# Hybrid decoder block: mLSTM values copied into the load tiles, and priority for the copies that empty the projection banks

## The chip, the cores and the metric

The kernel runs on one core of a Trainium2 chip. Its time is the device time of one execution in microseconds (us), as the median of several runs; lower is better. A profiled execution, one of its own, gives the instructions of each engine with their times: TensorE (PE, with its weight loads as PEld), VectorE (DVE), ScalarE (ACT), GpSimdE (POOL), and SyncE (SP), which here only issues transfers (DMA).

## The reference, cut to what matters

One decoder layer over 2048 tokens of width 1024, all in float32. One combined projection of the normalised input gives what two mixers need:

```python
h = modulate(rms_norm(x, g_pre_mix), shift_m, scale_m)
q_a, k_a, v_a, q_m, k_m, v_m, o_m, i_m, f_m, g_a, g_m = split(h @ w_in)
q_a, k_a = rope(q_a), rope(k_a)
y_a = sliding_window_attention(q_a, k_a, v_a, sinks)        # window 128, 8 query and 2 key heads of 64
q_m, k_m = silu(causal_conv(q_m, k_m))
h_m = mlstm_chunkwise(q_m, k_m, v_m, i_m + b_i, f_m + b_f)  # 4 heads of 128, values v_m
y_m = sigmoid(o_m) * head_layer_norm(h_m)
merged = sigmoid(g_a) * (y_a @ W_A) + sigmoid(g_m) * (y_m @ W_B)
x = x + gate * rms_norm(merged @ w_out);  then the same sandwich around a SwiGLU feed-forward
```

## The kernel before

The tokens are worked on in four blocks of 512 (`TB`), numbered 0 to 3, two of them to a superblock; a block has four token tiles of 128 (`NT`). Every product in float32 is made of three products of split operands (a high and a low part each), which `mm3` issues. The high part of a weight is a ScalarE copy (`split`, L264 and L267, L1744 in `split_unit`), the low part a VectorE subtraction (L268, L1745). Sums stand in banks of PSUM: four named acc for the projections, four named mix for everything smaller (transposes, attention, mLSTM).

Queries (`evac_q`, 512 columns), keys with attention values and mLSTM gates (`evac_kv`, 264 columns) and mLSTM values (`vm`, 512 columns) are projected by `token_group`: it takes the four acc banks at once, one for each token tile, goes through the eight slices of the weights in four pieces, and after the last piece calls `evac` for each token tile, which copies the bank to SBUF. The order in a superblock is: queries, keys and values of its first block (in the first superblock queries and keys of block 0 come in a part of its own, `first_block`, whose instructions are kept in the order written), then keys, queries and values of its second block. After that come the other columns (`om`, `qk`, `ga`, `gm`), by fast products of both blocks at once (`pair_parts`), whose results are sums of seven products and which again use the acc banks.

What becomes of the copies:

- Queries: the copy (L813) goes to a tx tile, VectorE turns it (rotary, L790 to L793), TensorE transposes it later (`q_stream`), and GpSimdE's queue stores it to DRAM (L806).
- Keys: the copy (L840) goes to a tx tile, for block 0 to an ld tile; the keys are turned, transposed in `k_stream` and stored (L833), the attention values are stored directly (L853) and as a difference to the tile before (L851), all on GpSimdE's queue.
- mLSTM values: the copy (L870) goes to a tx tile, and SP's queue stores it to DRAM (L871). The mLSTM loads it from there when its chunk's turn comes (L1084).

Tiles that share a tag share a fixed number of places in SBUF. tx has nine of them, for the copies above, for VectorE's work on them, for weights of the conditioning (`ada_stream`, L476) and much else. ld has four, `kvp.tile([P, 512], ...)`; besides the keys of block 0 they hold the queries and keys that the mLSTM loads for a chunk (L1079, L1082; the first at 374.6 us). A tile's place is given on when all that read it are through, a transfer out of it included.

The order of the instructions on an engine is not the order written, but for `first_block`. The kernel's own planner weaves work into the projections: generators (attention, gates, rotary parts, `hsums`, whose L575 and L576 split sums after a copy by transfer, L569) are given due times in its own count of TensorE time (`now`, `spawn`, `tick`). The framework then schedules what was written: it goes through a model of the chip in time, and each engine takes, of the instructions whose inputs and places are ready in the model, the one with the highest priority, which by default is the one written first. On the chip each engine then goes through its list in that order and waits where the model was too quick.

Of the kernel before, what the change touches and what calls it, by code (L numbers as in the profile page):

```python
# [19 lines left out]
P = 128  # L20
# [24 lines left out]
L_LOAD, L_HP2, L_HC = 5000.0, 1000.0, 3000.0  # L45
L_TANH, L_CONV, L_HD = 1500.0, 4000.0, 5000.0
L_LATE = 2500.0
L_KV0 = 0.0
L_HS2 = 4000.0
L_REST = (2000.0, 1800.0, 2500.0, 2500.0)  # L50
# [23 lines left out]
def decoder_block(ctx: ExitStack, tc: tile.TileContext, a: dict, out: bass.AP, dbg=None):  # L74
# [19 lines left out]
    V, A, T, Q = (InOrder(e) for e in (nc.vector, nc.scalar, nc.tensor, nc.sync))  # L94
# [19 lines left out]
    def nm(s):  # L114
        uid[0] += 1
        return f"{s}{uid[0]}"
# [7 lines left out]
    def tx(shape, dtype=F32):  # L124
        return tpool.tile(shape, dtype, tag="tx", name=nm("tx"), bufs=9)
# [88 lines left out]
    def transpose(o, i):  # L214
        now[0] += 110.0
        k = i.shape[0]
        T.transpose(o, i, ident[:k, :k])  # L217

    def spawn(gen, delay=0.0):
        st = [now[0] + delay, gen, False]  # L220
        streams.append(st)
        return st
# [116 lines left out]
    def token_group(srcs, nk, n, lhs, evac, pair_heads=False, stagger=1, store=None, kept=False):  # L339

        acc = []
        srcs = list(srcs)
        held = []

        def make(si, k0, kc):
            def mms(wt):
                if not acc:
                    acc.extend(acc_tile() for _ in range(NT))
                held.append((wt, k0, kc))
                if len(srcs) - stagger <= si < len(srcs) - 1:  # L350
                    return
                for t in range(NT):
                    for w_, k0_, kc_ in held:
                        for j in range(kc_):
                            kk = k0_ + j
                            mm3(acc[t][:, :n], lhs(kk, t), (w_[0][:, j, :], w_[1][:, j, :]), kk == 0, kk == nk - 1)
                            yield
                    if si == len(srcs) - 1:
                        evac(t, acc[t])
                held.clear()  # L360
            return mms

        for si, (raw, view, k0, kc) in enumerate(srcs):
            if kept:
                def ready(raw=raw, q=view):
                    return tuple(v.rearrange("p (k c) -> p k c", k=2) for v in raw.tile[q])
                yield Part(raw, ready, make(si, k0, kc))
                continue
            part = piece(raw, view, [kc, n], make(si, k0, kc), pair_heads)
            if store:  # L370
                def prep(do=part.prep, si=si, kc=kc):
                    made = do()
                    for i, v in enumerate(made):
                        nc.sync.dma_start(W_D[store][:, si, i, :].rearrange("p (k c) -> p k c", k=kc), v.bitcast(F32))
                    return made
                part.prep = prep
            yield part

    def srcs_rows(w, nk, c0):
        for k0 in range(0, nk, 4):  # L380
            kn = min(4, nk - k0)
            raw = raw_rows(w, k0, kn, c0)
            for j in range(0, kn, 2):
                yield raw, (lambda t, j=j: t[:, j:j + 2, :]), k0 + j, 2
# [350 lines left out]
    def ld(shape, dtype=F32):  # L735
        t = kvp.tile([P, 512], dtype, tag="ld", name=nm("ld"), bufs=4)
        return t.rearrange("p (k c) -> p k c", k=shape[0])
# [31 lines left out]
    def superblock(sb):  # L769
# [3 lines left out]
        def lhs_h(b):  # L773
            def lhs(kk, t):
                return tuple(p_[:, kk % 4, t * P:(t + 1) * P] for p_ in HC[f"{kk // 4 + 1}{b % 2 + 1}"])
            return lhs


        def rope(raw, heads, b, t):
            sin, cos = tables[sb]  # L780
            t += (b % 2) * NT
            W = heads * HD
            raw = raw[:, :W]
            src = raw.rearrange("p (h u f) -> p h u f", u=2, f=32)
            cb = cos[:, t, :].unsqueeze(1).to_broadcast([P, heads * 2, 32])
            sb_ = sin[:, t, :].unsqueeze(1).unsqueeze(1).to_broadcast([P, heads, 2, 32])
            z = tx([P, 512])
            zz = z[:, :W].rearrange("p (h u f) -> p h u f", u=2, f=32)
            rr = raw.rearrange("p (h f) -> p h f", f=32)
            V.tensor_tensor(zz, src[:, :, ::-1, :], sb_, op=ALU.mult)  # L790
            V.tensor_tensor(rr, rr, cb, op=ALU.mult)
            V.tensor_tensor(src[:, :, 0, :], src[:, :, 0, :], zz[:, :, 0, :], op=ALU.subtract)
            V.tensor_tensor(src[:, :, 1, :], src[:, :, 1, :], zz[:, :, 1, :], op=ALU.add)  # L793
            return raw, z

        def q_stream(b, t, yz):
            yield L_ROPE
            y, z = yz
            pt = mix_tile()
            for j in range(GQ):  # L800
                transpose(pt[:, j * P:(j + 1) * P], y[:, j * P:(j + 1) * P])
            hi, lo = z.bitcast(F32R), y.bitcast(F32R)
            A.activation(hi, pt, AF.Copy, scale=HD ** -0.5)
            V.scalar_tensor_tensor(lo, pt, HD ** -0.5, hi.bitcast(F32), op0=ALU.mult, op1=ALU.subtract)
            for i, q in enumerate((hi, lo)):
                G.dma_start(at_d[b * NT + t][:, i * 512:(i + 1) * 512], q.bitcast(F32))  # L806
# [3 lines left out]
        def evac_q(b):  # L810
            def evac(t, ps):
                raw = tx([P, 512])
                A.copy(raw, ps)  # L813
                R["qk"].append(spawn(q_stream(b, t, rope(raw, HQ, b, t))))
            return evac

# [6 lines left out]
        def k_stream(n, yz):  # L823
            yield L_ROPEK
            y, z = yz
            pt = mix_tile()
            transpose(pt[:, :P], y)
            kk = z[:, P:3 * P].bitcast(F32R).rearrange("p (i k) -> p i k", i=2)
            A.copy(kk[:, 0, :], pt[:, :P])
            V.tensor_tensor(kk[:, 1, :], pt[:, :P], kk[:, 0, :].bitcast(F32), op=ALU.subtract)  # L830
            for n_, u in ((n, 1), (n + 1, 0)):
                if n_ < S // P:
                    G.dma_start(at_d[n_][:, AT_K:AT_V].rearrange("p (i u k) -> p i u k", i=2, u=2)[:, :, u, :], kk.bitcast(F32))  # L833

        def evac_kv(b):
            before = [v_last]

            def evac(t, ps):
                raw = ld([1, 512])[:, 0, :] if b == 0 else tx([P, 392])
                A.copy(raw[:, :264], ps[:, :264])  # L840
                v, dv = raw[:, 128:256], raw[:, 264:392]
                n = b * NT + t
                y = rope(raw, HKV, b, t)
                for i in range(2):
                    A.copy(gt[:, t, 32 * i:32 * i + 4], raw[:, 256 + 4 * i:260 + 4 * i])
                V.tensor_tensor(dv, v, before[0], op=ALU.subtract)
                before[0] = v
                if t == NT - 1:
                    A.copy(v_last, v)
                    before[0] = v_last  # L850
                G.dma_start(at_d[n][:, AT_V + P:], dv)  # L851
                if n + 1 < S // P:
                    G.dma_start(at_d[n + 1][:, AT_V:AT_V + P], v)  # L853
                R["qk"].append(spawn(k_stream(n, y)))
            return evac
# [10 lines left out]

        def vm(b):
            def evac(t, ps):
                v = tx([P, 512])
                A.copy(v, ps)  # L870
                nc.sync.dma_start(vm_d[b][:, t, :], v)  # L871
            if b > 1:
                yield from token_group(kept_weights("vm"), KD, 512, lhs_h(b), evac, kept=True)
            else:
                yield from token_group(srcs_rows(w_in, KD, C_VM), KD, 512, lhs_h(b), evac, store="vm" if b else None)
# [477 lines left out]
        if sb == 0:  # L1353
            raws, rotated = {}, {}

            def late_q(t):
                yield from q_stream(b0, t, rope(raws[t], HQ, b0, t))

            def q_raw(t, ps):
                raws[t] = tx([P, 512])  # L1360
                A.copy(raws[t], ps)
                if t > 1:
                    R["qk"].append(spawn(late_q(t), L_KV0 + L_LATE * (t - 1)))

# [871 lines left out]
def build(nc, aps, out):  # L2236
    with tile.TileContext(nc, schedule_with_timeline_sim=True) as tc, ExitStack() as ctx:
        decoder_block(ctx, tc, aps, out[0])
# [16 lines left out]
```

## Time and profile before

| | |
|---|---|
| median of 3 runs | 2659.16 us (2657.73 to 2660.38) |
| profiled execution | 2668.66 us, span 2667.0 us |
| granted TensorE clock, mean | 0.994 |
| busy: PE, DVE, ACT, POOL | 2615.5, 1937.2, 1281.9, 300.3 us |
| DMA | 532.97 MB, mean 200 GB/s |

The profile page gives the busy time of each engine, the span in 40 slices, the chain of work that ended last, and the costliest groups of instructions. Views of the trace add the order in time of each engine's instructions (timeline: start and duration in us, engine, line, operation, tiles written and read; in brackets the idle time of the engine just before and what ended it), who waited for whom, and the busy time, the granted clock of TensorE and the busy share of the 16 DMA engines in chosen windows. A line such as L870 is line 870 of the kernel before. L212 is the helper that issues the matmuls, L217 the one for transposes; L90 is a helper for what is kept in program order. An "issue" as what ended a wait means that the view shows nothing that the engine waited for.

### The profile page before, as it was taken

How to read it: one execution, taken by the hardware profiler on the slowest of the kernel's cores; microseconds unless marked ns; L12 is line 12 of the kernel's file. 1: busy time of each engine (PE TensorE's matmuls, PEld its weight loads, DVE VectorE, ACT ScalarE, POOL GpSimd, SP SyncE). 2: the span in 40 equal slices, each digit the busy share in tenths (PEclk: the TensorE clock that was granted, in tenths of full speed). 3: DMA queues.
4: the chain of work that ended last, by engine and by line, in shares of the span. 5: the costliest groups of instructions: out<-in, count | busy, mean ns of one | idle time of the engine just before them, and what ended most of it. 6: DMA issues, size and time to landing. Idle time of an engine off the chain costs nothing.

```text
span 2667.0 us, 36229 instructions
## 1 busy us (share of the span) xinstructions
PE 2615.5 (98%) x12546; PEld 2145.8 (80%) x12546; DVE 1937.2 (73%) x3758; ACT 1281.9 (48%) x2531; POOL 300.3 (11%) x473
## 2 busy tenths in 40 slices
PE   8999999999989999999999999999999999999998
PEld 6877788888876788888878888888778888888876
DVE  5878887768676988875777777775776767676466
ACT  6656544545654654454643433345554333333444
POOL 0320001101132000210001111110000011001000
PEclk9899999999999999999999999999999999999999
DMA  7785465887787545597765554446675323234556
GB/s 270 255 303 164 135 196 183 291 301 253 262 313 244 166 135 181 183 296 268 220 238 193 184 169 153 163 139 228 213 242 173 111 99 116 90 111 139 199 196 220
DMA packets 327032, 532.97 MB, mean 200 GB/s; under 512 B 23136, under 2 KB 197724, under 8 KB 320064
## 3 DMA queue, kind: packets, MB, share of 16 engines
q1 hardware_dynamic: 287752, 448.45, 50.4%
q0 software_dynamic: 20880, 66.41, 6.6%
q10 hardware_dynamic: 18216, 15.79, 1.9%
q8 instruction: 99, 1.62, 0.2%
q14 instruction: 85, 0.70, 0.1%
HBM read 367.61 MB, written 154.57 MB: 196 GB/s over the span
## 4 chain that ended last, share of the span: by engine, by line
PE 88%; DVE 4%; DMA 3%; ACT 2%; issue 1%; POOL 0%; ACTq 0%; SPq 0%; DVEq 0%; POOLq 0%
PE acc L212 62%; PE mix L212 22%; PE mix L217 2%; PE acc L90 1%; DVE hl L1745 1%; PE mix L90 1%; DMA raw<-as_d 1%; ACT hl L1744 1%; DMA big<-big 0%; DMA raw<-ws_d 0%; DMA raw<-in_w_in_dram 0%; ACT tm L1002 0%; DMA at_d<-tx 0%; DMA raw<-in_w_ffn_down_dram 0%; ACT big L575 0%
## 5 line engine op out<-in xcount | busy, mean ns | idle before, releaser
L212 PE MATMUL acc<-big,hl 128*128 128x512 f32 x3936 | 936.4, 393 | 7.0 <-ACT tx L870 5.4
L212 PEld LDWEIGHTS acc<-big,hl 128*128 128x128 f32 x3936 | 733.8, 188 | 166.4 <-ACT tx L870 5.9
L1744 ACT CAST hl<-raw 128x512 fp32r<-128x512 f32 x732 | 439.9, 621 | 489.6 <-PE acc L212 208.7
L1745 DVE TENSOR_TENSOR hl<-raw,hl 128x512 fp32r<-128x512 f32 x732 | 495.1, 692 | 198.4 <-ACT hl L1744 196.0
L212 PE MATMUL acc<-whi,big 128*128 128x512 f32 (+1 forms) x896 | 281.6, 390 | 3.0 <-ACT tx L870 3.0
L212 PE MATMUL mix<-big,hl 128*128 128x512 f32 x1056 | 263.0, 390 | 1.8 <-ACT hl L1744 1.1
L212 PE MATMUL acc<-hl,hl 128*128 128x512 f32 x1008 | 237.2, 393 | 6.2 <-DVE hl L1745 3.3
L212 PEld LDWEIGHTS mix<-big,hl 128*128 128x128 f32 x1056 | 197.8, 188 | 44.5 <-ACT hl L1744 2.0
L212 PEld LDWEIGHTS acc<-hl,hl 128*128 128x128 f32 x1008 | 187.1, 188 | 51.8 <-DVE hl L1745 8.8
L212 PEld LDWEIGHTS acc<-whi,big 128*128 128x128 f32 x896 | 168.6, 192 | 36.2 <-ACT tx L870 3.4
L212 PE MATMUL mix<-hl,hl 128*128 128x512 f32 x792 | 182.7, 391 | 3.4 <-ACT hl L1744 2.6
L212 PEld LDWEIGHTS mix<-hl,hl 128*128 128x128 f32 x792 | 147.8, 188 | 37.6 <-ACT hl L1744 4.2
L212 PE MATMUL acc<-wlo,big 128*128 128x512 f32 (+1 forms) x448 | 174.4, 389 | 0.0
L212 PE MATMUL acc<-big,whi 128*128 128x512 f32 x512 | 157.3, 393 | 0.0
L268 DVE TENSOR_TENSOR wlo<-raw,whi 128x1024 fp32r<-128x1024 f32 (+1 forms) x76 | 90.8, 1194 | 65.7 <-ACT whi L267 60.2
L267 ACT CAST whi<-raw 128x1024 fp32r<-128x1024 f32 (+1 forms) x76 | 78.4, 1032 | 109.7 <-PE acc L212 103.5
L492 POOL TENSOR_TENSOR rs<-ms,halves 128x1 f32<-128x1 f32 (+1 forms) x56 | 41.3, 744 | 797.8 <-DVE ms L490 750.4
L212 PE MATMUL mix<-hcT4h,hl 128*128 128x512 f32 x352 | 115.6, 389 | 0.7 <-ACT hl L1744 0.7
L212 PE MATMUL acc<-hcT2h,hl 128*128 128x512 f32 x352 | 115.5, 389 | 0.0
L212 PEld LDWEIGHTS acc<-big,whi 128*128 128x128 f32 x512 | 95.3, 188 | 19.3
L212 PEld LDWEIGHTS acc<-wlo,big 128*128 128x128 f32 x448 | 85.8, 192 | 18.0 <-issue 1.2
L212 PE MATMUL acc<-big,wlo 128*128 128x512 f32 x256 | 97.6, 392 | 0.0
(388 smaller groups left out, 3802.3 us busy)
## 6 DMA issues: line engine op xcount, KB each, us to landing
as_d<-w POOLq DMA_DIRECT2D x154, 256.0 KB, 2.5
raw<-in_w_in_dram SPq DMA_DIRECT2D x36, 1024.0 KB, 5.4
raw<-as_d SPq DMA_DIRECT2D x70, 512.0 KB, 3.8
raw<-in_w_ffn_gate_dram SPq DMA_DIRECT2D x22, 1024.0 KB, 6.1
raw<-in_w_ffn_up_dram SPq DMA_DIRECT2D x22, 1024.0 KB, 5.8
raw<-ws_d SPq DMA_DIRECT2D x40, 512.0 KB, 4.6
tx<-in_w_ada_dram SPq DMA_DIRECT2D x64, 256.0 KB, 5.3
g_d<-tx SPq DMA_DIRECT2D x64, 256.0 KB, 2.4
```

The source lines that it names most:

```text
L90: self.last = tc.keep_in_program_order(f(*p, **k)).ins
L212: T.matmul(o, lhsT=lhsT, rhs=rhs, start=start, stop=stop, skip_group_check=resumed)
L217: T.transpose(o, i, ident[:k, :k])
L267: A.copy(hv, src)
L268: V.tensor_tensor(lv, src, hv.bitcast(F32), op=ALU.subtract)
L492: G.tensor_tensor(r[:, :n], ms[:, :n], nhalf[:, :n], op=ALU.pow)
L1744: A.copy(v(hi), src)
L1745: V.tensor_tensor(v(lo), src, v(hi).bitcast(F32), op=ALU.subtract)
```

## The change

The values of the mLSTM are copied to an ld tile instead of a tx tile, and three kinds of copies (queries outside `first_block`, keys of all blocks, values) are written under a higher priority: as if each stood 2000 instructions earlier in the text. Tiles, stores and the other instructions of these steps are written where they were.

```diff
+EARLY = 2000
...
+    def leave(dst, src):
+        with tc.high_priority(offset=EARLY):
+            A.copy(dst, src)
...
         def evac_q(b):
             def evac(t, ps):
                 raw = tx([P, 512])
-                A.copy(raw, ps)
+                leave(raw, ps)
...
             def evac(t, ps):
                 raw = ld([1, 512])[:, 0, :] if b == 0 else tx([P, 392])
-                A.copy(raw[:, :264], ps[:, :264])
+                leave(raw[:, :264], ps[:, :264])
...
         def vm(b):
             def evac(t, ps):
-                v = tx([P, 512])
-                A.copy(v, ps)
+                v = ld([1, 512])[:, 0, :]
+                leave(v, ps)
                 nc.sync.dma_start(vm_d[b][:, t, :], v)
```

## The prediction, made before the kernel was run

> **What bounds the kernel now.** I read the page first (its engine line and the chain that ended last), then the list of waits for TensorE, which tells what little TensorE still waits for, and then the timelines and windows of the places in that list that the change touches.
>
> ```profile
> PE 2615.5 (98%) x12546; PEld 2145.8 (80%) x12546; DVE 1937.2 (73%) x3758; ACT 1281.9 (48%) x2531; POOL 300.3 (11%) x473
> ```
>
> TensorE is busy 2615.5 us of a span of 2667.0, so a change to ScalarE's order can win no more than TensorE's idle time and what that idle time does to its clock. The waits of TensorE, longest first, columns total us, times, longest:
>
> ```profile
> PE acc L212 <- ACT tx L870: 8.4, 4, 4.6
> PE mix L90 <- DMA tm<-in_mlstm_norm_w_dram: 5.1, 1, 5.1
> ```
>
> The longest entry is a copy that the change moves: L870 empties a bank of mLSTM values. It holds TensorE four times, 8.4 us in all. L813 (queries) and L840 (keys) have no row there; this is what the 40 copies cost and, for L813, who waits:
>
> ```profile
> L870 ACT COPY tx<-acc x16: 575/587/596, 95.4 to 870.4; 128x512 f32<-128x512 f32 x16
> ...
> L813 ACT COPY tx<-acc x12: 578/588/647, 149.1 to 838.7; 128x512 f32<-128x512 f32 x12
> ...
>   DVE tx L790: 9.2, 2
> ...
> L840 ACT COPY tx<-acc x12: 358/380/426, 124.6 to 780.5; 128x264 f32<-128x264 f32 x12
> ```
>
> So the change is worth something at three places at most: near 105 us (block 0 to block 1), near 192 and near 858 us.
>
> **Place A, 104 to 121 us.** The timelines of TensorE and ScalarE, and those of GpSimdE's and SP's issues, each with the time to landing of single issues (us, last column):
>
> ```profile
> 102.65 1.84 PE L212 MATMUL mix<-at 64*128 64x128 f32 x24
> 104.80 0.39 PE L212 MATMUL acc<-whi,big 128*128 128x264 f32 x1 [0.31 <-ACT tx L870]
> ...
> 108.97 0.59 PE L212 MATMUL acc<-whi,big 128*128 128x264 f32 x1 [2.69 <-ACT tx L870]
> ```
>
> ```profile
> 104.18 0.57 ACT L870 COPY tx<-acc 128x512 f32<-128x512 f32 x1
> 108.34 0.59 ACT L870 COPY tx<-acc 128x512 f32<-128x512 f32 x1 [3.58 <-issue]
> ```
>
> ```profile
> 98.73 0.73 POOL L833 DMA_DIRECT2D at_d<-tx  x1 [4.69 <-issue]
> 99.46 0.55 POOL L851 DMA_DIRECT2D at_d<-ld  x1
> ...
> at_d<-tx POOLq DMA_DIRECT2D x1, 128.0 KB, 9.5
> at_d<-ld POOLq DMA_DIRECT2D x1, 64.0 KB, 9.5
> ```
>
> ```profile
> 95.96 1.31 SPq L871 DMA_DIRECT2D vm_d<-tx  x2
> ...
> vm_d<-tx SPq DMA_DIRECT2D x1, 256.0 KB, 8.7
> ```
>
> The last copy of the block starts at 108.34, after 3.58 us in which ScalarE waited for nothing that the view names. GpSimdE's store of a tx tile, issued at 98.73, takes 9.5 us: 108.2. I read the wait as that for a free tx tile, not for ScalarE's time. What follows the stall is dearer than the stall; windows of 3.41 us, or 13.65, around it and around the two later stalls:
>
> ```profile
> core 0: us, PE busy (x) PEld busy (x) DVE busy (x) ACT busy (x) POOL busy (x), PEclk, DMA share, GB/s
> 104.41:107.82 3.41, 1.56 (x11) 1.27 (x10) 3.37 (x7) 0.34 (x1) 0.00 (x0) 1.00 1.00 382
> 107.82:121.47 13.65, 12.23 (x59) 11.36 (x60) 9.21 (x25) 7.89 (x25) 3.22 (x6) 0.50 0.96 326
> 121.47:124.88 3.41, 3.41 (x25) 3.10 (x26) 2.53 (x14) 2.51 (x9) 1.77 (x2) 1.00 0.02 7
> 855.30:858.70 3.40, 0.00 (x0) 0.00 (x0) 1.57 (x4) 1.65 (x4) 0.00 (x0) 1.00 1.02 425
> 858.70:862.10 3.40, 3.38 (x8) 2.71 (x9) 3.40 (x8) 3.40 (x8) 0.00 (x0) 0.51 0.99 416
> 862.10:865.50 3.40, 3.40 (x16) 2.79 (x16) 3.40 (x7) 1.83 (x4) 0.00 (x0) 0.99 1.08 392
> ```
>
> After a window in which TensorE was busy 1.56 of 3.41 us the granted clock is 0.50 for 13.65 us, with TensorE busy for 12.23 of them: 12.23 / 2 = 6.1 us lost. After 858.70 it is half for one window only (1.7 us).
>
> **The change, part by part.** (1) *Cost of the copies.* 40 copies before, 40 after, same shapes: nothing added. (2) *mLSTM values into ld tiles.* Only the tile's pool changes; the store L871 stays on SP. At A the values then need one of four ld tiles, which the keys of block 0 hold. Three of those are let go early (only one store from an ld tile is as late as 99.46), so the third copy goes as soon as its products are done, before 104.18, and the 0.31 stall goes. The fourth copy takes whichever tile is let go first: the one of the last keys (99.46 + 9.5 = 108.96) or the one that the first value copy itself used, whose store was issued at 95.96 and landed 8.7 later: 104.66. I take the second, the earlier of the two. The copy then ends at 104.66 + 0.59 = 105.25; TensorE, without the 0.31, wants the bank at 108.97 - 2.69 - 0.31 = 105.97. Both stalls go: 3.0 us. The window from 104.41 is then full like the one from 121.47, which ran at 1.00, so I take the clock as kept: 6.1. Together 9.1; the other end is -0.6 (108.96 + 0.59 against 108.34 + 0.59).
>
> (3) *What the gain meets next.*
>
> ```profile
> 125.00:160.00 35.00, 35.00 (x187) 26.73 (x186) 24.47 (x73) 19.92 (x58) 12.31 (x18) 1.00 0.98 347
> 160.00:185.00 25.00, 25.00 (x141) 19.49 (x140) 17.98 (x41) 18.61 (x56) 4.71 (x4) 1.00 0.79 287
> 185.00:200.00 15.00, 12.96 (x72) 9.27 (x71) 14.79 (x28) 8.16 (x15) 4.92 (x9) 1.00 0.71 231
> ```
>
> In the next 35 us the DMA engines are 0.98 busy. If all those bytes must land in the stage, TensorE can leave it only 0.02 x 35 = 0.7 us earlier; if the stores among them may slide on, the following 40 us have 25 x 0.21 + 15 x 0.29 = 9.6 us free and all 9.1 is kept (TensorE was busy 35.00 of 35.00 there, so no load was late). Neither row decides; I keep half: 4.55. Ends 0.7 and 9.1.
>
> (4) *Places B and E (192 and 858 us), and one where I count nothing.*
>
> ```profile
> 191.87 0.58 ACT L870 COPY tx<-acc 128x512 f32<-128x512 f32 x1
> ...
> 857.05 1.14 ACT L1744 CAST hl<-raw 128x512 fp32r<-128x512 f32 x2 [8.55 <-DMA raw<-in_w_in_dram]
> 858.09 1.07 ACT L870 COPY tx<-acc 128x512 f32<-128x512 f32 x2
> ```
>
> ```profile
> 187.38 0.66 PE L217 MATMUL mix<-ident,tx 128*128 128x128 f32 x4 [1.22 <-DVE tm L1035]
> ...
> 192.50 0.73 PE L212 MATMUL acc<-big,hl 128*128 128x512 f32 x2 [0.82 <-ACT tx L870]
> ...
> 766.18 6.15 PE L212 MATMUL acc<-raw,big 128*128 128x264 f32 x36 [4.18 <-ACT tm L985]
> ...
> 858.72 1.65 PE L212 MATMUL acc<-big,hl 128*128 128x512 f32 x3 [4.55 <-ACT tx L870]
> ```
>
> The weight loads at these places, of 1 MB each: from the chain of waits (start, us), from the SP queue, and its time to landing:
>
> ```profile
> 845.62 11.34 DMA raw<-in_w_in_dram
> ...
> 752.22 1.46 SPq L333 DMA_DIRECT2D raw<-w_kv_d  x1
> ...
> raw<-w_kv_d SPq DMA_DIRECT2D x1, 1056.0 KB, 13.8
> ```
>
> B: no key holds an ld tile in block 1, the copy goes when its bank is full, and the 0.82 goes; the 1.22 just before (a wait for VectorE) might be filled with the same products, which I leave to the range. E: the view names L870, but ScalarE stood 8.55 us behind a weight load that landed at 845.62 + 11.34 = 856.96. The first split ends at 857.05 + 0.57, so TensorE could start at about 857.7 instead of 858.72: 1.0 us, and the rest of the 4.55 stays, with its window of half clock. With priority the values' stores go out some us earlier, while that load is under way; two of them, 512 KB at the row's 425 GB/s, could put it off by 1.2 us: the gain there is 1.0, ends -0.2 and 1.0. At 766.18 the view names ScalarE, but the keys' weights, issued at 752.22, land 13.8 later, at 766.02: a DMA wait, nothing to win.
>
> (5) *Priority of queries and keys.* TensorE never waits for L813 or L840; VectorE's 9.2 us lie beside a full TensorE. Worth nothing. Each copy that overtakes another instruction delays it by 0.59 or 0.38 us; the work overtaken is above all weight splits, which themselves wait for TensorE:
>
> ```profile
> L267 ACT CAST whi<-raw 128x1024 fp32r<-128x1024 f32 x72 | 75.9, 1054 | 102.1 <-PE acc L212 96.0 <-issue 4.9 <-ACT tm L605 1.1
> ```
>
> With that cover gone it would cost a stall of 0.59 at each of a few places.
>
> **Sum.** 4.55 + 0.82 + 1.0 = 6.4 us off. The profiled execution took 2668.66 us (its span plus 1.7), so it would be 2662.3; the median shown is 2659.16, 9.5 lower, and there the forecast is **2652.8 us**.
>
> **A rule weighed.** The Trainium skill (TensorE: Matmul & The Clock Gate, "What's actually happening") says that the clock halves after an idle window of about 3.4 us and comes back after one busy window. Row and rule differ twice at A: the window before the drop was 1.56 us busy, and the half clock lasted four windows, not one; at 858.70 the rule holds. By the rule, a stall that stays at A after the change costs 1.7 us of clock instead of 6.1, which is the third rival below.
>
> **Rivals.**
> 1. *The fourth copy waits for the last keys' ld tile* (108.96). A gives -0.6, B and E stay: 1.2 off, 2658.0. For it: the tile is one of only four; against it: 104.66 is earlier. Chance 0.25.
> 2. *Everything kept, and the 1.22 at B filled*: 9.1 + 2.0 + 1.0 = 12.1 off, 2647.1. Chance 0.16.
> 3. *The stall stays, the clock does not*: as rival 1, but half clock for one window (as at 858.70), 4.4 us won: 5.6 off, 2653.6. Needs TensorE's order behind the stall free of small products. Chance 0.07.
> 4. *Slower.* As rival 1, and the priority also puts the waiting copy further ahead in ScalarE's order: all behind it (attention's queries L803, the splits L575 and L267) stands until 108.96, and TensorE then stalls from before the 24 small attention products that now run at 102.65, which it has still to do at 108.96 (1.8 us) with the products behind the 0.31. 0.6 + 1.8 + 0.3 + one more window of half clock (1.7) = 4.4, and 8.8 where a second block does the same; I take 6 between the two: 2665. It decides as soon as the tile comes later than 108.3. Chance 0.13.
> 5. *No effect*: the copies already come first when they are ready, and the values only change one full pool for another: 2659. Chance 0.07.
>
> **How the numbers follow.** Forecast 0.32. The measurement can tell about 0.2% (5.3 us) from no change. Faster: three quarters of the forecast's 0.32, rivals 2 and 3: 0.47. Within 0.2%: the rest of it, rivals 1 and 5: 0.40. Slower 0.13. The range reaches from rival 2's end (2646.5) past rivals 1 and 5 to half of rival 4 (2662.5); the forecast's own case is 2649 to 2657.
>
> **What would show it.** Right: no wait of TensorE named L870 near 105 and 192 us; granted clock 1.00 in 105 to 121 us; values' copies there starting at once after their products; near 858 TensorE still idle for some 3.5 us, now behind the weight load. Wrong: a copy L870 (then into ld) that starts near 109 after a wait that no engine ends; the half clock of 13.65 us still there or moved; or TensorE waiting for weights in 115 to 160 us, which would mean that the DMA engines took all of A back.

## The result: slower by 0.24%

The changed kernel takes 2667.74 us in the median of 9 runs (2666.66 to 2670.71), the kernel before 2660.28 in 9 runs beside it (2657.73 to 2665.70). The ratio is 1.0024, 95% interval 1.0016 to 1.0032: slower by 6 to 7 us, where 6.4 less were forecast. The profiled execution of the changed kernel took 2666.66 us (span 2665.0), 1.1 us under its median. The profile of the kernel before, from which the prediction was worked out, stood 9.5 us above its own.

Lines of the changed kernel are 5 higher than before (matmuls L213 for L212, the value copies are now L222, `leave`). Its page, engine line:

```profile
PE 2615.9 (98%) x12546; PEld 2146.1 (81%) x12546; DVE 1940.8 (73%) x3758; ACT 1282.5 (48%) x2531; POOL 299.9 (11%) x473
```

The busy times are those of before: the same work, in another order. The list of TensorE's waits after the change (us in total, times, longest):

```profile
PE acc L213 <- ACT hl L1749: 6.2, 6, 3.2
PE acc L213 <- DVE hl L1750: 6.0, 5, 3.0
...
PE mix L218 <- DVE tm L917: 2.8, 1, 2.8
...
PE acc L213 <- ACT big L580: 0.8, 1, 0.8
PE acc L213 <- ACT tx L222: 0.8, 1, 0.8
```

The 8.4 us behind the value copies are gone from the list (0.8 is left, for a key copy at 123 us). In their place stand the split weights (hl, L1749 and L1750) and the gates of VectorE (L917). Windows of TensorE's clock around A (near 112 us) and E (near 855 us), after the change:

```profile
109.74:113.15 3.41, 2.14 (x23) 1.97 (x24) 3.29 (x10) 0.84 (x4) 0.00 (x0) 1.00 1.06 393
113.15:116.56 3.41, 3.41 (x16) 3.41 (x17) 3.04 (x10) 2.01 (x5) 0.00 (x0) 0.50 0.93 313
843.61:847.02 3.41, 0.83 (x8) 0.52 (x6) 0.00 (x0) 0.07 (x1) 0.00 (x0) 1.00 1.05 404
847.02:853.85 6.83, 6.23 (x15) 4.93 (x16) 6.18 (x12) 4.23 (x8) 1.62 (x3) 0.50 1.02 419
857.26:860.67 3.41, 0.50 (x1) 0.19 (x1) 3.37 (x8) 2.19 (x5) 0.00 (x0) 1.00 1.08 375
860.67:867.50 6.83, 6.09 (x14) 4.79 (x15) 5.65 (x12) 2.17 (x4) 0.00 (x0) 0.50 0.75 300
```

At A the half clock is down from 13.65 us to 3.41. At E it is up from 3.41 to 13.66, in two spells, each behind a window in which TensorE was busy 0.83 or 0.50 of 3.41 us. In the third and fifth row VectorE is the engine to look at: 0.00 busy, then full.

### The profile page after: what moved, and what is told of

Same layout as the page of the kernel before. It is cut to its first block, busy times and chain, and to the rows that moved or that the text cites. A ratio compares the mean times of both kernels' runs of the same rounds, so it can differ in the third digit from the quotient of the medians.

```text
span 2665.0 us, 36227 instructions
## 1 busy us (share of the span) xinstructions
PE 2615.9 (98%) x12546; PEld 2146.1 (81%) x12546; DVE 1940.8 (73%) x3758; ACT 1282.5 (48%) x2531; POOL 299.9 (11%) x473
## 4 chain that ended last, share of the span: by engine, by line
PE 90%; DVE 4%; DMA 3%; ACT 1%; issue 1%; POOL 0%; ACTq 0%; SPq 0%; DVEq 0%; POOLq 0%
PE acc L213 63%; PE mix L213 23%; PE mix L218 2%; PE acc L91 1%; DVE hl L1750 1%; PE mix L91 1%; DMA raw<-as_d 1%; ACT hl L1749 1%; DMA raw<-w_kv_d 1%; DMA raw<-ws_d 0%; DMA big<-big 0%; DMA raw<-in_w_in_dram 0%; DMA raw<-in_w_ffn_down_dram 0%; DVE big L1750 0%; DMA wlo<-w_vm_d 0%
## 5 line engine op out<-in xcount | busy, mean ns | idle before, releaser
L213 PE MATMUL acc<-big,hl 128*128 128x512 f32 x3936 | 941.6, 394 | 8.5 <-ACT hl L1749 3.9
L213 PEld LDWEIGHTS acc<-big,hl 128*128 128x128 f32 x3936 | 736.8, 189 | 168.7 <-ACT hl L1749 5.5
L1749 ACT CAST hl<-raw 128x512 fp32r<-128x512 f32 x732 | 440.0, 621 | 491.2 <-PE acc L213 218.2
L1750 DVE TENSOR_TENSOR hl<-raw,hl 128x512 fp32r<-128x512 f32 x732 | 498.4, 697 | 200.8 <-ACT hl L1749 198.3
L213 PE MATMUL acc<-whi,big 128*128 128x512 f32 (+1 forms) x896 | 281.0, 388 | 0.9 <-ACT tx L222 0.8
L213 PE MATMUL mix<-big,hl 128*128 128x512 f32 x1056 | 262.9, 390 | 1.8 <-ACT hl L1749 1.1
L213 PE MATMUL acc<-hl,hl 128*128 128x512 f32 x1008 | 237.4, 393 | 5.4 <-DVE hl L1750 3.0
L213 PEld LDWEIGHTS mix<-big,hl 128*128 128x128 f32 x1056 | 197.8, 188 | 44.4 <-ACT hl L1749 2.0
L213 PEld LDWEIGHTS acc<-hl,hl 128*128 128x128 f32 x1008 | 187.0, 188 | 51.1 <-DVE hl L1750 8.6
L213 PEld LDWEIGHTS acc<-whi,big 128*128 128x128 f32 x896 | 167.2, 189 | 35.1 <-issue 1.2
L213 PE MATMUL mix<-hl,hl 128*128 128x512 f32 x792 | 182.8, 391 | 2.9 <-ACT hl L1749 1.9
L213 PEld LDWEIGHTS mix<-hl,hl 128*128 128x128 f32 x792 | 147.8, 188 | 37.2 <-ACT hl L1749 3.6
L213 PE MATMUL acc<-wlo,big 128*128 128x512 f32 (+1 forms) x448 | 173.4, 388 | 0.6 <-DMA wlo<-w_vm_d 0.6
L213 PE MATMUL acc<-big,whi 128*128 128x512 f32 x512 | 157.3, 393 | 0.0
L213 PE MATMUL mix<-hcT4h,hl 128*128 128x512 f32 x352 | 115.6, 389 | 0.7 <-ACT hl L1749 0.7
L213 PE MATMUL acc<-hcT2h,hl 128*128 128x512 f32 x352 | 115.5, 389 | 0.0
L213 PEld LDWEIGHTS acc<-big,whi 128*128 128x128 f32 x512 | 95.3, 188 | 19.4
L213 PEld LDWEIGHTS acc<-wlo,big 128*128 128x128 f32 x448 | 85.0, 190 | 18.3 <-issue 1.2
L213 PE MATMUL acc<-big,wlo 128*128 128x512 f32 x256 | 97.6, 392 | 0.0
```

The source lines that it names most:

```text
L213: T.matmul(o, lhsT=lhsT, rhs=rhs, start=start, stop=stop, skip_group_check=resumed)
L1749: A.copy(v(hi), src)
L1750: V.tensor_tensor(v(lo), src, v(hi).bitcast(F32), op=ALU.subtract)
```

## The experiments

Each was timed beside the kernel before; the median is given, and the ratio to before with its 95% interval. The kernel's 103 executions beside the first sixteen experiments lie between 2656.05 and 2667.58, median 2662.0.

**The kernel before, profiled again.** No edit.

> The kernel before, unchanged, profiled and timed again. Theory P (the profile of before that the prediction was worked out from was an unlucky execution, 8.4 us above its own median): median 2660 +- 1.5, and the new profiled execution, at about 2659, shows at most 6.8 us of half clock between 105 and 125 us instead of 13.65. Theory Q (the 13.65 us of half clock belong to the kernel): they are there again, and the profiled time is again near 2668, or the 8 us less are found at another place.

Measured: 2662.25 us, ratio 1.0004 (0.9995 to 1.0012); profiled execution 2661.69, span 2660.0. Its windows at the two places:

```profile
110.26:113.67 3.41, 2.10 (x23) 1.92 (x23) 3.33 (x8) 0.84 (x3) 0.00 (x0) 1.00 0.96 306
113.67:117.08 3.41, 3.41 (x16) 3.41 (x17) 2.53 (x10) 3.38 (x12) 0.00 (x0) 0.50 1.07 378
...
854.36:857.77 3.41, 3.41 (x10) 2.69 (x9) 3.41 (x9) 3.41 (x9) 0.00 (x0) 0.50 1.00 423
```

One window of half clock at A, not four: theory P. The 6.1 us that the prediction found in the clock at A were mostly an accident of one execution. TensorE's waits at A in this profile:

```profile
107.07 0.39 PE L212 MATMUL acc<-whi,big 128*128 128x264 f32 x1 [1.53 <-ACT tx L870]
...
111.57 0.44 PE L217 MATMUL mix<-ident,tm 68*128 68x68 f32 x4 [2.06 <-DVE tm L912]
```

Behind the copy stands a second wait, for the last VectorE instruction of the gates; in the first profile it was 0.27 us.

**The changed kernel again.** No edit.

> The changed kernel again, timed and profiled a second time. If its 13.7 us of half clock between 847 and 868 belong to it, at least 10 us of them are there again, and the ratio is again 1.002 to 1.003. If they were chance like the 13.65 us near 108 in the first profile of before: 7 us or less, and the time lies with the shorter executions, 2663 or less.

Measured: 2667.97, ratio 1.0023 (1.0014 to 1.0032), 13.66 us of half clock between 847 and 868. It belongs to the kernel.

With two profiles of the changed kernel and an ordinary one of before, the loss can be placed: TensorE's stalls (every one over 0.06 us), plus half of its busy time at half clock, added up from its timeline and the windows (us).

```
                     before, again      after            after, again
60-140   (A)         3.6 + 1.7 =  5.3   3.7 + 1.7 =  5.4   3.8 + 3.4 =  7.2
140-250  (B)         2.1                0                  0
700-800              7.8 + 1.7 =  9.5   5.1 + 2.5 =  7.6   5.6 + 2.5 =  8.1
800-900  (E)         4.9 + 1.7 =  6.6   7.8 + 6.2 = 13.9   9.4 + 5.1 = 14.5
900-1300             0                  1.2                1.4
all the rest         21.5               22.2               21.6
sum                  44.9               50.3               52.7
span                 2660.0             2665.0             2665.9
```

E loses 7 to 8 us, more than the whole difference of the spans (5.0 and 5.9); B and the stretch from 700 to 800 give back 3.5 to 4. The sums differ by 5.4 and 7.8, so the account is good to about 2 us.

**Each edit alone, and each half.** Load tiles alone; priority alone; both in blocks 0 and 1 alone:

```diff
-                v = tx([P, 512])            # e2: A.copy stays
+                v = ld([1, 512])[:, 0, :]
...
-                A.copy(raw, ps)             # e3: leave() at all three places, v stays in tx
+                leave(raw, ps)
...
+        if b < 2:                           # e4: leave() and ld only there
```

> mLSTM values into load tiles, no priority. If the loss of the change comes with the priority: 2654 to 2660, the stall near 105 us gone. If it comes with the load tiles (values hold tiles that weight or attention loads want): about 2667.

> Priority for the copies of queries, keys and mLSTM values, the values still in tx tiles. If the loss comes with the priority, which brings the values' stores and the next stage's loads into another order: about 2667, with more than 10 us of half clock between 845 and 870 us. If it comes with the load tiles: 2658 to 2661, and the wait for a free tx tile near 109 us still there (some 2.7 us).

> Both edits for token blocks 0 and 1 only; blocks 2 and 3 are copied as before. Theory S (the loss arises behind 750 us, where the profile after shows 13.7 us of half clock between 847 and 868 against 3.4 before): 2655 to 2660, half clock near 860 us back to one window of 3.41. Theory F (the loss arises in the first two blocks, before 200 us, or by chance anywhere): 2664 to 2668.

Measured: 2665.87 (ratio 1.0016, 1.0007 to 1.0025), 2669.05 (1.0027, 1.0015 to 1.0038) and 2665.49 (1.0012, 1.0003 to 1.0022). Each part alone is slower, and they do not add up. The load tiles alone have the three stalls of the changed kernel (3.54, 0.83 and 2.83 us at 851 to 863); priority alone has seven smaller ones (0.5 to 1.9 us) between 848 and 889 instead. With blocks 0 and 1 alone E is one stall and one window, as theory S had it, but the time is not back: it was half right.

**Block 3's values alone; all but these; block 3's queries alone; blocks 0 to 2 without priority.**

```diff
+                v = ld([1, 512])[:, 0, :] if b == 3 else tx([P, 512])   # e5; e12: if b < 3
+                (leave if b == 3 else A.copy)(v, ps)                     # e5; e12: if b < 3, queries and keys as in the change
...
+                (leave if b == 3 else A.copy)(raw, ps)                   # e13: in evac_q only
...
+                v = ld([1, 512])[:, 0, :] if b < 3 else tx([P, 512])     # e16: A.copy everywhere
```

> Both edits for the mLSTM values of token block 3 alone; everything else as before. Theory E (most of the loss arises where block 3 ends: the value copies run and store early, the second half's weights come some 6 us sooner, and the gates' chain of VectorE then falls between the splits of those weights, so that TensorE stalls three times near 847, 858 and 861 us and the clock halves again): three stalls there again, half clock of 6.8 us or more between 845 and 870 where before has 3.41, and 2664 to 2667. Theory D (the loss is dispersed: any change of the order costs some us somewhere): near 858 as before, time anywhere from 2660 to 2668.

> The changed kernel, with block 3's mLSTM values alone copied as before (tx tile, no priority). If the values of block 3 are what brings the three stalls near 848 to 862: one stall of 4 to 5 us there and one window of half clock, 2659 to 2663. If queries and keys with priority do it: three stalls as in the changed kernel, 2666 to 2669.

> The kernel before with priority for the copies of block 3's queries alone. In the written-out order of the engines the priority of all other query and key copies moves no TensorE instruction, and that of block 3's queries moves 276. Theory Q (this is all the priority does): the stalls between 845 and 890 as with priority alone (1.3, 0.9, 0.6, 1.0, 1.9 in place of one of 4.4), 2665 to 2670. If the priority acts elsewhere: 2660 to 2663.

> Values of blocks 0, 1 and 2 in load tiles, no priority; against the kernel before this one it tells what place A costs. Theory V (at A the gates' chain sets the time; the split of one stall into two windows is lost, so that the clock halves for 6.8 us in place of 3.4): A gives nothing and costs one more window, 2 us above the kernel with blocks 1 and 2. If the values at A were worth what the prediction said: 3 to 9 us below it.

Measured: 2672.24 (1.0040, 1.0027 to 1.0052); 2666.79 (1.0018, 1.0010 to 1.0027); 2669.35 (1.0031, 1.0021 to 1.0041); 2662.60 (1.0003, 0.9994 to 1.0012). Around the last one they form a square:

```
values of blocks 0-2 in ld tiles, and for block 3:    values as before    values in ld
    queries without priority                          2662.6 (e16)        2665.9 (e2)
    queries with priority                             2666.8 (e12)        2667.7, 2668.0 (the change)
```

In this square the loss comes with block 3: either edit brings 3 to 4 us, both together 5, and the load tiles of the three earlier blocks cost and bring nothing when all three are changed. The effects do not add up beyond the square: block 3's values alone cost 10 us, its queries alone 7. (The lower row has the priority of all copies. With the values in tx tiles, TensorE's order with all priorities (e3) is that with block 3's queries alone (e13), so no other query or key copy moves an instruction there; with the values in load tiles the values' priority also moves some in earlier blocks.) The fourth kernel missed its expectation at A: it is not 2 us above the kernel with blocks 1 and 2 below, but 4 under it.

The traces place this without the other blocks' share. The edits of block 3 change TensorE's order only from its 4281st to its 4933rd instruction (826 to 953 us in the kernel before, again). Against that profile TensorE loses over this stretch 7.8 and 8.3 us in the change, 6.4 in the load tiles alone, 10.0 in block 3's values alone, 3.4 to 3.6 with the priority (e3, e12, e13), and between -1.0 and 2.6 in the six kernels that leave block 3 as before and its gates in place. For the priority the list of waits does not show all of it: in e13 waits and half clock between 800 and 900 come to 7.7 us, only 1.1 more than before. In e3 and e13 a further 4.4 us go near 1389 us, at a wait of 1.9 us for ScalarE and a window of half clock that the kernel before (again) does not have; why is open.

**What the two edits of block 3 have in common.** The timelines of TensorE and VectorE, before (profiled again), where TensorE uses up block 3's products and the second half's first weights are on their way (the gates begin with four transposes on TensorE, mix<-ident,gt, then go on on VectorE):

```profile
843.02 0.60 PE L217 MATMUL mix<-ident,gt 128*36 128x128 f32 x4
...
853.95 7.36 PE L212 MATMUL acc<-big,hl 128*128 128x512 f32 x24 [4.40 <-ACT tx L870]
```

```profile
843.66 0.68 DVE L899 COPY tm<-mix 4x512 f32<-4x512 f32 x1 [2.99 <-PE mix L217]
...
845.58 1.35 DVE L905 TENSOR_TENSOR_SCAN tm<-ones,tm 4x128 f32<-4x128 f32 x4
...
849.44 0.42 DVE L912 TENSOR_SCALAR tm<-tm 4x512 f32<-4x512 f32 x1
...
852.29 0.69 DVE L1836 TENSOR_TENSOR tx<-raw 128x512 f32<-128x512 f32 x1 [2.21 <-DMA raw<-in_w_in_dram]
```

and after the change:

```profile
843.84 0.60 PE L218 MATMUL mix<-ident,gt 128*36 128x128 f32 x4
```

```profile
847.60 0.69 DVE L1750 TENSOR_TENSOR hl<-raw,hl 128x512 fp32r<-128x512 f32 x1 [5.66 <-ACT hl L1749]
...
849.53 0.68 DVE L904 COPY tm<-mix 4x512 f32<-4x512 f32 x1
...
852.05 1.35 DVE L910 TENSOR_TENSOR_SCAN tm<-ones,tm 4x128 f32<-4x128 f32 x4
853.33 1.25 DVE L914 TENSOR_TENSOR_SCAN tm<-tm,m_last,tm 4x512 f32<-4x512 f32 x1
...
857.71 0.42 DVE L917 TENSOR_SCALAR tm<-tm 4x512 f32<-4x512 f32 x1
...
861.29 0.67 DVE L1750 TENSOR_TENSOR hl<-tx,hl 128x512 fp32r<-128x512 f32 x1
```

Before, VectorE does the gates of block 3 (L899 to L912) while TensorE still has products and the weights travel, and waits 2.21 us for the weights. After, the transposes are the last thing TensorE does before it runs out, and the first splits stand ahead of the gates in VectorE's order. It is idle for 5.66 us; the gates could have run from 844.44, when their transposes end, that is for the last 3.2 of these. Then it does them between the splits that TensorE needs:

```profile
847.62 9.50 PE L213 MATMUL acc<-big,hl 128*128 128x512 f32 x26 [3.18 <-ACT hl L1749]
857.95 0.50 PE L213 MATMUL acc<-big,hl 128*128 128x512 f32 x1 [0.83 <-ACT big L580]
861.41 10.61 PE L213 MATMUL acc<-big,hl 128*128 128x512 f32 x33 [2.96 <-DVE hl L1750]
```

The weights come sooner as well, for their load is issued 4.1 us earlier, before again and after:

```profile
842.72 0.41 SPq L1908 DMA_DIRECT2D raw<-in_w_in_dram  x1
```

```profile
838.58 0.38 SPq L1913 DMA_DIRECT2D raw<-in_w_in_dram  x1
```

TensorE starts the second half's products at 847.62, where the kernel before starts them at 853.95, and then stands twice. VectorE's idle time directly ahead of those weights tells the kernels with an edit in block 3 from the others: 2.1 and 2.2 us at 2662.6 and 2662.25; 5.5, 5.7, 6.3, 8.0, 8.1, 8.3 and 8.6 us in the load tiles alone, the change (twice), block 3's queries alone, priority alone, all but block 3's values, and block 3's values alone, all of them at 2665.9 or more. (The kernels that change blocks 0 to 2 but not 3 have 1.5 to 3.1 us there; what they lose, up to 10 us, they lose elsewhere.) It is a mark of the order and not the size of the loss: the kernel before is also idle for 2.99 us just ahead of the gates, 5.2 us in all.

**That order made in the kernel before, without touching a copy; and unmade in the changed one.**

```diff
-            yield L_GATE
+            yield L_GATE + (2600.0 if b == 3 else 0.0)     # e17, in the kernel before
...
+            keep(V.tensor_copy(lf, pg[32:36, :]))          # e18, in the changed kernel: block 3's gates and then
+            ...                                            # the first four splits, in the order written
```

> The kernel before, with the gates' chain of block 3 written 2.6 us later, so that in VectorE's order it stands behind the splits that wait for the second half's first weights, as in the changed kernel; no copy is touched. Theory H (VectorE, in order, stands idle behind those weights for 6 to 8 us and lacks this time in the 80 us after, so TensorE waits there): VectorE idle over 5 us near 845 to 853, its busy time in 840 to 880 down from 33.9 to about 28 to 30, and 2666 to 2670. Rival (VectorE's idle there costs nothing; the loss comes from the copies): 2660 to 2664.

> The changed kernel, with the gates' chain of block 3 kept ahead of the first splits of the second half's weights on VectorE, as it stood in the kernel before; the splits of the sums then also stand ahead of the first weights' split. Theory H: VectorE works on the gates while the weights are on their way, one stall of TensorE (4 to 7 us) in place of three, one spell of half clock, VectorE busy 32 or more of 840 to 880; 2661 to 2665. Rival: three stalls again or the same time, 2666 to 2670.

Measured: 2670.79 (1.0035, 1.0023 to 1.0048) and 2684.43 (1.0082, 1.0068 to 1.0097). VectorE in the first:

```profile
852.00 0.69 DVE L1836 TENSOR_TENSOR tx<-raw 128x512 f32<-128x512 f32 x1 [7.29 <-DMA raw<-in_w_in_dram]
...
863.49 0.68 DVE L899 COPY tm<-mix 4x512 f32<-4x512 f32 x1
```

7.29 us idle, and 9 us lost, with every copy written as before; 7.9 of them go in the stretch from 826 to 953 us. The edit puts the gates later as a whole, their transposes on TensorE too (at 862.5 us), so the gates were not yet to be had in these 7.29 us. VectorE's busy time from 840 to 880, before again, after, and in this kernel (third column of busy times, after PE and PEld):

```profile
840.00:880.00 40.00, 35.60 (x186) 28.51 (x185) 33.91 (x78) 20.53 (x54) 3.22 (x6) 0.96 0.81 292
```

```profile
840.00:880.00 40.00, 32.89 (x145) 25.34 (x144) 29.50 (x56) 18.21 (x35) 3.25 (x6) 0.83 0.84 298
```

```profile
840.00:880.00 40.00, 35.57 (x176) 27.97 (x175) 27.96 (x53) 17.34 (x36) 3.24 (x6) 0.91 0.82 294
```

33.91, 29.50 and 27.96: the 4.4 and 6 us are made up later, beside TensorE. Here TensorE pays most at 889.64 (2.88 us of wait for a split, 6.83 us of half clock), not at 861. That this delay comes from the gates fits the busy times, but is not shown step by step: the split waited for stands behind attention work on ScalarE.

The second kernel missed its expectation and did not unmake the loss. VectorE did the gates (849.42 to 853.85), then splits of the sums, and only then the first weight's split, and TensorE stood 8.07 us for it:

```profile
853.85 0.67 DVE L586 TENSOR_TENSOR big<-big,big 128x512 fp32r<-128x512 f32 x1
...
856.65 0.67 DVE L1757 TENSOR_TENSOR hl<-raw,hl 128x512 fp32r<-128x512 f32 x1
```

```profile
857.38 4.28 PE L213 MATMUL acc<-big,hl 128*128 128x512 f32 x10 [8.07 <-DVE hl L1757]
```

VectorE had no idle time from 848.81 until that split, so this kernel shows a cost of VectorE's order, but not one of idle time behind a late load. The weights were there at 846.66, and gates that can start only at 844.79 hold their splits up when they go first.

**Gates of block 3 later in the changed kernel; gate copies on ScalarE.**

```diff
+            yield L_GATE + (4000.0 if b == 3 else 0.0)                # e10
...
-            V.tensor_copy(lf, pg[32:36, :])                            # e8, and L906
+            A.copy(lf, pg[32:36, :])
```

> The changed kernel; the gates' chain of block 3 is put 4 us later in the written order, so that VectorE does it behind the splits of the second half's first weights instead of between them. Theory E (that chain is what keeps TensorE at 858 to 863 us): the stall of 3.0 us near 861 goes or falls below 1, the half clock between 856 and 868 goes, only the stall for the weights near 848 stays; 2659 to 2663. Rival W (the splits wait for weights and ScalarE; VectorE would be late anyway): stalls of 0.8 and 3.0 stay, 2666 to 2669.

> The changed kernel, with the two 4x512 copies that begin the gates' chain (0.68 us each on VectorE) moved to ScalarE. If VectorE's chain is what TensorE waits for near 111 and 861 us: the 2.8 us stall near 111 shrinks by 0.7 to 1.4, the one near 861 (3.0) by as much, one or two windows of half clock fewer, 2661 to 2665. If the waits come from elsewhere (weights, splits on ScalarE): stalls as before, 2666 to 2669.

Measured: 2669.35 (1.0025, 1.0015 to 1.0036) and 2667.06 (1.0023, 1.0014 to 1.0032). TensorE in the first:

```profile
850.78 15.59 PE L213 MATMUL acc<-big,hl 128*128 128x512 f32 x55 [4.06 <-ACT hl L1749]
...
906.25 0.66 PE L218 MATMUL mix<-ident,tm 128*128 128x128 f32 x4 [0.88 <-POOL tm L1010]
909.55 3.03 PE L213 MATMUL acc<-big,hl 128*128 128x512 f32 x9 [2.19 <-DVE hl L1750]
```

The waits of 0.83 and 2.96 us at 858 and 861 are gone, as theory E had it, which speaks for the gates as what stood in between. But the time is not won: 3.1 us of waits and a window of half clock come at 906, where VectorE is busy 39.78 of the 40 us from 880 to 920 with what was put off. In the second kernel the wait for VectorE's split is down to 1.70 us (at 864), the clock is 1.00 from 840 to 880 and TensorE busy 37.5 of 40. At A its expectation failed: the stall for the gates grew to 3.56 us. Others are now at 269 (2.53) and 786 us (3.04).

**Place A alone, and the gates of block 0.**

```diff
+                v = ld([1, 512])[:, 0, :] if b == 0 else tx([P, 512])   # e7, with leave() for b == 0
...
+            gcopy = A.copy if b in (0,) else V.tensor_copy               # e9 in the kernel before;
+            if not b: rw = tm([68, TB]); G.memset(rw, 0.0)               # ahead of yield L_GATE; e11: in the change, with e10's edit
```

> Both edits for the mLSTM values of token block 0 alone (place A of the prediction). Theory V (at A VectorE's chain of gates sets the time, not the bank's copy): the wait for the copy near 107 us goes, but TensorE stalls 2.5 to 3.5 us for the gates' last VectorE instruction near 109 to 112 us, in place of 1.5 + 2.1 us; time 2661 to 2664. Theory of the prediction (the copy sets it): no stall over 0.5 us between 104 and 115 us; time 2656 to 2659.

> The kernel before; in block 0 alone the two copies that begin the gates' chain go to ScalarE and the clearing of that chain's tile (GpSimdE) is put ahead of them. Theory V (near 105 to 115 us TensorE waits for the chain of gates; a faster copy of the values alone cannot help): the chain's last instruction comes 1.4 to 2 us sooner, the stall of 2.1 us at 111 becomes 0.7 or less; the wait for the value copy (1.5) stays; one window of half clock fewer in most executions: 2657 to 2661. If the order of other work matters more: 2662 to 2670.

> The changed kernel with both: block 0's gates as in the first kernel of this set, block 3's gates later as in the second. Theories V and E together: no stall over 1.5 us between 104 and 115, none for VectorE near 861, 2655 to 2660, below both kernels. If either falls: 2662 to 2668.

Measured: 2672.24 (1.0044, 1.0030 to 1.0057), 2672.75 (1.0038, 1.0025 to 1.0050) and 2667.36 (1.0020, 1.0011 to 1.0029). TensorE at A in the first:

```profile
111.05 0.69 PE L217 MATMUL mix<-ident,tm 68*128 68x68 f32 x4 [2.83 <-DVE tm L916]
...
124.83 0.50 PE L212 MATMUL acc<-whi,big 128*128 128x512 f32 x1 [0.91 <-ACT tx L844]
```

The copy's wait is gone and the gates' wait has grown from 2.06 to 2.83: theory V at its place. With a shorter chain of gates it shrank to 0.24 us (second kernel) and 1.90 (third), as V says in kind, though the third kernel's stall is above the 1.5 expected. No time came of it: the first kernel loses 9 us between 100 and 400 us, the second stalls 3.19 us at 185 and halves its clock for 6.83 there, the third stalls 4.80 us for VectorE at 856.

**Place B alone, and blocks 1 and 2.** The line of e16 with `b == 1` and `b in (1, 2)`.

> The kernel before with block 1's mLSTM values alone in load tiles. Place B of the prediction alone: if its 2.1 us of stalls near 183 and 189 go and nothing else moves: 2659 to 2661 (1 to 3 below before). If they only move (to 200 or to 760): 2661 to 2668.

> Values of blocks 1 and 2 in load tiles, blocks 0 and 3 as before, no priority: the changed kernel without the two places that lost. If B's 2.1 us and the 2 us that the profile after is better by between 750 and 800 are kept: 2656 to 2660, below both kernels. If any change of the order between 750 and 800 brings another stall there: 2661 to 2667.

Measured: 2664.50 (1.0009, 1.0000 to 1.0018) and 2666.45 (1.0018, 1.0009 to 1.0027). B's stalls go (0.4 and 0.5 us are left of 2.1), and the time is no better. Both have 6.83 us of half clock at E, with one stall of 4.9 and 4.5 us, which takes back 3 to 5 us of the gain. But in the profile of the second kernel TensorE is still 1.6 us ahead of the kernel before (again) at 1300 us; 4.3 us go at 1385, at a wait of 2.51 us for ScalarE and a window of half clock, and the rest after 1800. None of the sixteen variants was faster than the kernel before.

## Why the prediction was wrong

The forecast was 2652.8 (2646.5 to 2662.5); 2667.74 was measured. By its steps:

1. *What bounds the kernel.* Right: TensorE's idle time and its clock are all that moved.
2. *Place A.* The mechanics were right to 0.9 us. The fourth copy took the tile of the first value copy:

```profile
103.81 0.59 ACT L222 COPY ld<-acc 128x512 f32<-128x512 f32 x1 [0.70 <-DMA vm_d<-ld]
```

   It starts at 103.81 (forecast 104.66), and no wait of TensorE there names it. "Both stalls go: 3.0 us" failed: TensorE then waits for the gates.

```profile
111.01 0.44 PE L218 MATMUL mix<-ident,tm 68*128 68x68 f32 x4 [2.83 <-DVE tm L917]
```

   In the profile that the prediction read, the copy had been so late that it hid this second wait. 1.53 + 2.06 before against 2.83 + 0.81 after: nothing won. The 6.1 us of clock were not the kernel's: 1.7 in the second profile, 1.7 and 3.4 after.
3. *Half kept.* Without meaning, as nothing was won.
4. *B, E, and 766.* B was right and too low: 2.06 won for 0.82. Near 766, where nothing was counted, 1.4 to 1.9 us were won. E is the step that failed most: +1.0 was forecast, "ends -0.2 and 1.0", and it cost 7.3 to 7.9. The step looked at one load and the copy behind it, and took the load's time as fixed. The load was issued 4.1 us earlier, and the gates that VectorE had done while it travelled came between the splits. The step did not ask which other work VectorE does in that time, and whether it still stands ahead of the splits once the order is made anew.
5. *Priority worth nothing.* Failed in block 3: 3.4 to 3.6 us between 826 and 953 (4.2 from e16 to e12 in the whole time). The step priced the work overtaken on ScalarE; the new order moved TensorE's and VectorE's work too. VectorE's gates stand behind the weights here as well, but which waits make up the loss is not shown.
6. *The sum.* Subtracting 6.4 from the median carried the terms of an execution 9.5 us above it to executions that do not have them. The profile's excess sat in the very place that the change was to mend; 6.1 of the 7.0 us between its two spans are half clock (11.2 and 5.1 us lost). Besides, the three runs that gave 2659.16 lay low: 2662.0 over 103 executions.

The slower rival was right in sign and near in size (2665), but not its mechanism: it wanted the tile later than 108.3, and it came at 103.8. The Trainium skill (TensorE: Matmul & The Clock Gate, "What's actually happening") says that the clock's windows run free of the kernel, so that one kernel's count of slow matmuls differs between executions. The traces agree: the two profiles of before lost 11.2 and 5.1 us to the clock with stalls of 42.3 and 39.8 us.

What stays open: that late gates of block 3 are enough to cost 8 to 9 us is shown by e17, and that they stand in the way at E by the timelines and by e10; how they turn into TensorE's waits 15 to 60 us later is not shown as a sum. That the change would lose nothing without them is not shown, as no version was found in which the changed kernel has its gates ahead of the weights with all else left alone. A rival stands beside it: nearly every new order cost some us somewhere, also those that leave block 3 alone (up to 10 us), so the order of before may simply be one that is hard to better.

## What to carry to other kernels

Before a stall is priced from a profile, hold its execution against the median: where the profile is slower than the runs by as much as the change is to bring, the stall may be the accident, and a second profile is worth more than any sum. When an edit makes the scheduler write the orders anew, look at every in-order engine where a large load is awaited, and ask what it does meanwhile and what will be queued behind the wait; that the copies' own engine is idle does not settle it. A stall taken away shows the next wait behind it, here the gates 4 us later, so look for the next-latest wait of the same stretch before a stall is priced.

## What the runs showed of the hardware

The clock's windows lie on a grid of 3.41 us that is set differently in each execution. Over the 20 profiles, all 61 full-clock windows between 40 and 2640 us in which TensorE was busy under 1.5 of 3.41 us were followed by half clock; of some 100 with 1.5 to 2.25 us, 26 were; above that, 1 of about 14,900. So in these profiles a stall of 2 to 3 us halved the clock or did not, by where the grid lay. The half clock then lasted one window (46 spells, up to 1.7 us lost in each) or two (38), four times longer, 13.65 us twice. The kernel before took 2656 to 2668 us over 103 executions; between its two profiles 6.1 of 7.0 us are half clock, and what the rest of the spread comes from is not shown.
